# A fused decoder layer: block turns on VectorE over a DRAM scratch in place of TensorE transposes, and a longer second half of the last accumulation

## The chip, the cores and the metric

The kernel runs on one core of a Trainium2 chip. The metric is the device time of one execution in microseconds (us). All weights stream from DRAM once per execution; nothing is kept from one execution to the next.

## The reference, cut to what matters

One layer of a decoder on 256 tokens with 2048 features, in float32: a mixer (a state-space part and a gated short convolution), a cross-attention to 256 memory tokens, a SwiGLU block with 5632 hidden features, plain residual sums, and an RMS norm at the end.

```python
mem_n = rmsnorm(mem, mem_norm)
h = x
h = h + hybrid_mixer(rmsnorm(h, norm_mix), w_in, ..., w_out)        # ends with [y_ssd, y_sc] @ w_out
h = h + memory_cross_attention(rmsnorm(h, norm_xa), mem_n, w_q, w_k, w_v, w_o)
h = h + swiglu(rmsnorm(h, norm_ffn), w_gate, w_up, w_down)          # (silu(h @ w_gate) * (h @ w_up)) @ w_down
return rmsnorm(h, norm_final)
```

## The kernel before

**Products in two parts.** Each float32 operand is split into a rounded part `h` and a rest `l`, and a product is three matmuls: activation-h by weight-h, activation-h by weight-l, activation-l by weight-h (L796 to L798 in `tok_mm`).

**The weight stream.** All weights come as one list of chunks of 128x1024 (512 KB), in the order in which they are used. SP loads a chunk into one of six raw buffers (L151). ScalarE rounds it into one of four `hi` buffers (L165), and VectorE subtracts to give one of four `lo` buffers (L166). A raw buffer is free again when its `lo` is written; a `hi` or `lo` buffer is free when TensorE has used its chunk.

**Units and steps.** `unit` takes two chunks: it issues the loads up to five chunks past the unit, the splits that are still due, the matmuls of the first chunk, then calls `step()`, which lets every waiting post-process go on to its next `yield`, then the matmuls of the second chunk and one more load. So a `yield` puts off what follows by one unit. The orders of TensorE and SP are as written here (`manual_schedule`); those of ScalarE and VectorE come from a planner that simulates the program and takes what is ready.

**Stages around the change.** The mixer's output product (`wo`) runs over four column groups n of 512 features, 16 chunks each. After each, `wo_post` adds the product to the residual `res[tb][n]` (two token blocks of 128) and, one unit later, `to_features` turns it into features by tokens for the query product: eight TensorE transposes of 128x128 (L823) and a scaled split into slots (L179, L180). Then come queries, attention by head (`scores`, `turn`, `values`), the attention's output product, and eleven groups of gate and up products (`g`, `u`, eight chunks each). `u_post` multiplies the gate by the up product (L1008) and one unit later turns the result with eight transposes (L1015) and splits it (L1018, L1019) into `gs`, which is the stationary operand of the down product `d`, four column groups of 22 chunks.

**The end.** In the last two chunks of a column group of `d`, token block 0 runs first and then token block 1. For the last group `d_last` follows each: sums and squares (`d_sums`), the scale (`d_scale`), and the scaled output (`d_out`) written by eight transfers of 256 KB. Before the change the outputs of block 0 are issued in the call for block 1, after block 1's squares.

Of the kernel before, what the change touches and what calls it, by code (L numbers as in the profile page):

```python
# [13 lines left out]
F32 = mybir.dt.float32  # L14
F32R = mybir.dt.float32r
AF = mybir.ActivationFunctionType
ALU = mybir.AluOpType
# [3 lines left out]
T = 256  # L21
# [68 lines left out]
def trunk(tc, wst, vecs, xp, xtp, mp, wdt_in, nfin, outp):  # L90
    nc = tc.nc
# [8 lines left out]
    with ExitStack() as ctx:  # L100
# [5 lines left out]
        sp = E(tc.tile_pool(name="slots", bufs=65))  # L106
        tp = E(tc.tile_pool(name="tmp", bufs=8))
        gtp = E(tc.tile_pool(name="gate", bufs=4))
        accp = E(tc.tile_pool(name="acc", bufs=4, space=PSUM))
        mscp = E(tc.tile_pool(name="msc", bufs=4, space=PSUM))  # L110
        drp = E(tc.tile_pool(name="scr", bufs=1, space=DRAM))
# [18 lines left out]
        def msc():  # L130
            return mscp.tile([128, 512], F32, tag="m", name=nm("m"))
# [41 lines left out]
        def v(name, i):  # L173
            return vec[:, VOFF[name] + i:VOFF[name] + i + 1]

        def hilo_scaled(src, gain):

            a = slot(dt=F32R)
            act(a[:, 0:T], src, AF.Identity, scale=gain)  # L179
            stt(a[:, T:], src, gain, a[:, 0:T].bitcast(F32), ALU.mult, ALU.subtract)  # L180
            return a
# [631 lines left out]
                j = gtp.tile([128, 512], F32, tag="g", name=nm("j"))  # L813
                act(j, h, AF.Square, accum_out=sums[:, tb, n:n + 1])

        def to_features(n, gain, dst):

            for i in range(2):
                ps = msc()
                for f in range(2):  # L820
                    for tb in range(2):
                        o = (2 * i + f) * 128
                        nc.tensor.transpose(ps[:, f * T + tb * 128:f * T + tb * 128 + 128],  # L823
                                            res[tb][n][:, o:o + 128], ident)
                for f in range(2):
                    t = 4 * n + 2 * i + f
                    dst[t] = hilo_scaled(ps[:, f * T:f * T + T], v(gain, t))

        def token_scale(name, sums, factor=None):

# [13 lines left out]
        def wo_post(n, accs):  # L844
            add_to_res(n, accs, h1s)
            if n == 0:
                act(small("rv"), half, AF.Exp)
            if n == 3:
                xa["sc"] = token_scale("xsc", h1s, XSCALE)
            yield  # L850
            to_features(n, "nxa", h1g)

        for n in range(4):
            accs = [acc(), acc()]
# [41 lines left out]
        def turn(h):  # L896
            p, pt = ps_[h], msc()
            for mb in range(2):
                for lb in range(2):
                    nc.tensor.transpose(pt[:, mb * T + lb * 128:mb * T + lb * 128 + 128],  # L900
                                        p[:, lb * T + mb * 128:lb * T + mb * 128 + 128], ident)
            pts[h] = slot()
            nc.scalar.copy(pts[h], pt)

        def values(h):
            op = msc()
# [9 lines left out]
        def o_post(n, accs):  # L916
            add_to_res(n, accs, h2s)
            if n == 3:
                ff["r"] = token_scale("fscale", h2s)
            yield  # L920
            to_features(n, "nffn", h2g)

        oacc = {}

# [78 lines left out]
        def u_post(n, accs):  # L1003
            while n not in gate:
                yield
            for tb in range(2):
                s = gate[n][tb]
                stt(s, accs[tb], ff["r"][:, tb:tb + 1], s, ALU.mult, ALU.mult)  # L1008
            yield
            for i in range(2):  # L1010
                ps = msc()
                for f in range(2):
                    for tb in range(2):
                        o = (2 * i + f) * 128
                        nc.tensor.transpose(ps[:, f * T + tb * 128:f * T + tb * 128 + 128],  # L1015
                                            gate[n][tb][:, o:o + 128], ident)
                hi, lo = slot(dt=F32R), slot(dt=F32R)
                nc.scalar.copy(hi, ps)  # L1018
                tt(lo, ps, hi.bitcast(F32), ALU.subtract)  # L1019
                gs[2 * n + i] = hi, lo  # L1020

        def f_mm(accs, m, n, c):
# [45 lines left out]
                act(j[:, c], h[:, c], AF.Square, accum_out=ss[:, tb, 3 + i:4 + i])  # L1068

        def d_scale(tb):  # L1070
            h, r = res[tb][3], fr[:, tb:tb + 1]
            stt(r, ss[:, tb, 3:4], 1.0 / D, pre[:, tb:tb + 1], ALU.mult, ALU.add)
            stt(r, ss[:, tb, 4:5], 1.0 / D, r, ALU.mult, ALU.add)  # L1073
            gtt(r, r, half[:, 0:1], op=ALU.pow)  # L1074
            tt(h, h, gain[3], ALU.mult)

        def d_out(tb, ns):
            r = fr[:, tb:tb + 1]
            for n in ns:
                h = res[tb][n]  # L1080
                if n == 1:
                    act(h, h, AF.Identity, scale=r)
                else:
                    ts(h, h, r, None, ALU.mult)
                (nc.scalar if n % 2 else nc.sync).dma_start(outp[tb][:, n * 512:n * 512 + 512], h)

        def d_last(tb, ps):
            engines = {mybir.EngineType.Activation, mybir.EngineType.DVE, mybir.EngineType.Pool}
            with tc.manual_schedule(engines=engines):
                d_sums(tb, ps)  # L1090
                if tb == 0:
                    d_scale(0)
                else:
                    d_out(0, (0, 1, 2))
                    d_scale(1)
                    d_out(0, (3,))
                    d_out(1, (0, 1, 2, 3))

        def d_mm(ps, key, tbs, start, stop):
# [6 lines left out]
            tok_mm(ps, key, blocks, tbs, start, stop)  # L1106

        nd = FT // 2
        for n in range(4):
            accs = [acc(), acc()]  # L1110
            for c in range(0, nd - 2, 2):
                unit([([("d", n, k)], lambda k=k: d_mm(accs, ("d", n, k), (0, 1), k == 0, False))
                      for k in (c, c + 1)])
            tail = [("d", n, nd - 2), ("d", n, nd - 1)]

            def last_mm(tb):
                for key in tail:
                    d_mm(accs, key, (tb,), False, key == tail[1])
# [10 lines left out]
def _pairs(a):  # L1129
    import numpy as np  # L1130
    return np.ascontiguousarray(a.T.reshape(8, 2, 128, T).transpose(0, 2, 1, 3).reshape(8, 128, 512))


def _cols(a):
# [7 lines left out]
def _weights(i):  # L1142
    import numpy as np
    w_in = np.asarray(i["w_in"])[0]
    blk = {}

    def tiles(w, ck):
        k, n = w.shape
        return w.reshape(k // 128, 128, n // 128, 128).transpose(2, 1, 0, 3)

    blk["a"] = tiles(w_in[:, 0:5120], 8)
    blk["b"] = tiles(w_in[:, 5152:], 8)
    blk["q"] = tiles(np.asarray(i["w_q"])[0], 8)
    rows = {m: np.asarray(i[k])[0].reshape(-1, 2, 128, i[k].shape[-1] // 512, 512).transpose(3, 0, 2, 1, 4)
            for m, k in (("wo", "w_out"), ("o", "w_o"), ("g", "w_gate"), ("u", "w_up"), ("d", "w_down"))}
    wk, wv = np.asarray(i["w_k"])[0], np.asarray(i["w_v"])[0]
    plan = stream_plan()
    out = np.empty(sum(128 * w for _, w in plan), np.float32)
    p = 0
    for key, w in plan:  # L1160
        m = key[0]
        if m == "k0":
            c = wk[0:128]
        elif m == "v0":
            c = wv[0:128]
        elif m == "kv":
            s = slice(key[1] * 128, key[1] * 128 + 128)
            c = np.concatenate([wk[s], wv[s]], axis=1)
        elif m in rows:
            c = rows[m][key[1], key[2]]  # L1170
        else:
            c = blk[m][key[1]][:, 8 * key[2]:8 * key[2] + w // 128]
        out[p:p + 128 * w] = c.reshape(-1)
        p += 128 * w
    return out


def _vectors(i):
    import numpy as np
    g = {k: np.asarray(a) for k, a in i.items() if a.ndim <= 3}  # L1180
    part = {
        "nmix": _cols(g["norm_mix"][0]), "nmem": _cols(g["mem_norm"]), "nxa": _cols(g["norm_xa"][0]),
        "nffn": _cols(g["norm_ffn"][0]), "nssd": _cols(g["ssd_norm"][0]),
        "nsc": _cols(g["sc_norm"][0]), "cw": _cols(g["ssd_conv_w"][0].T), "cb": _cols(g["ssd_conv_b"][0]),
        "sw": _cols(g["sc_conv_w"][0].T), "dsk": _cols(np.repeat(g["d_skip"][0], 64)),
        "dtb": np.broadcast_to(g["dt_bias"][0], (128, H)), "alog": np.broadcast_to(g["a_log"][0], (128, H)),
    }
    return np.ascontiguousarray(np.concatenate([part[n] for n, _ in _W], axis=1))
# [33 lines left out]
```

## Time and profile before

| | us |
|---|---|
| median of 3 runs (1557.65 to 1558.63) | 1558.58 |
| the profiled execution | 1558.37 |
| span of its instructions | 1556.7 |
| TensorE busy / VectorE busy / ScalarE busy | 1541.9 / 916.8 / 805.3 |
| DMA, mean over the span | 193 GB/s |

The profile shows one execution. Its time is 1.7 us longer than the span, which goes from the first to the last instruction. Busy time of TensorE counts matmuls whose ends are modelled and which overlap; the distance between two starts tells what one costs.

### The profile page before, as it was taken

The numbers are of one execution on the slowest core, as the hardware profiler recorded it, in microseconds if no ns is written. First come the engines' busy times: TensorE is split into PE (matmuls) and PEld (weight loads), VectorE is DVE, ScalarE is ACT, GpSimd is POOL, SyncE is SP. The second block draws the span as 40 slices with busy tenths as digits, with TensorE's granted clock in tenths as the row PEclk, the third lists the DMA queues.
The fourth block names the chain that finished last, engine by engine and source line by source line (L and its number), as shares of the span: only waits on it lengthen the run. The fifth ranks groups of instructions, "written<-read, shape, count | busy, mean of one in ns | idle before, by whom it ended". The sixth has DMA issues, their size and how long they took to land.

```text
span 1556.7 us, 20300 instructions
## 1 busy us (share of the span) xinstructions
PE 1541.9 (99%) x7716; PEld 1294.6 (83%) x7716; DVE 916.8 (59%) x1214; ACT 805.3 (52%) x1157; POOL 46.6 (3%) x65
## 2 busy tenths in 40 slices
PE   9999999999999999999999999999999999999997
PEld 7888888888888888888888888888888888888886
DVE  5976886776776674555575555545455555455453
ACT  6685775774765454444465444444444444344342
POOL 0011300100000000000000000000000000000000
PEclk9999999999999999999999999999999999999999
DMA  9665655655655556665545555555555556656662
GB/s 346 248 199 192 217 173 181 209 183 173 220 170 183 173 186 199 203 202 202 191 134 183 189 184 193 189 197 189 189 189 188 183 194 209 201 191 195 194 191 95
DMA packets 92962, 300.66 MB, mean 193 GB/s; under 512 B 9888, under 2 KB 18496, under 8 KB 92864
## 3 DMA queue, kind: packets, MB, share of 16 engines
q1 hardware_dynamic: 83664, 291.98, 56.4%
q10 hardware_dynamic: 9200, 7.39, 1.6%
q8 instruction: 60, 0.98, 0.2%
q14 instruction: 38, 0.31, 0.1%
HBM read 297.19 MB, written 2.15 MB: 192 GB/s over the span
## 4 chain that ended last, share of the span: by engine, by line
PE 96%; DMA 2%; ACT 1%; DVE 0%; issue 0%; SPq 0%; POOLq 0%; POOL 0%; DVEq 0%; ACTq 0%
PE a L294 21%; PE a L796 20%; PE a L798 20%; PE a L797 20%; PE a L300 11%; DMA s<-in_m_dram 1%; PE m L1015 1%; PE m L674 1%; DMA r<-in_w_dram 0%; PE m L823 0%; PE m L200 0%; ACT h L165 0%; DMA s<-in_x_dram 0%; PE m L242 0%; PE a L516 0%
## 5 line engine op out<-in xcount | busy, mean ns | idle before, releaser
L166 DVE TENSOR_TENSOR l<-r,h 128x1024 fp32r<-128x1024 f32 (+2 forms) x555 | 657.2, 1193 | 537.0 <-ACT h L165 464.4
L165 ACT CAST h<-r 128x1024 fp32r<-128x1024 f32 (+2 forms) x555 | 564.5, 1022 | 629.2 <-PE a L798 475.3
L796 PE MATMUL a<-h,s 128*128 128x512 f32 x1344 | 525.7, 391 | 0.0
L798 PE MATMUL a<-h,s 128*128 128x512 f32 x1344 | 523.2, 389 | 0.0
L797 PE MATMUL a<-l,s 128*128 128x512 f32 x1344 | 523.0, 389 | 0.0
L294 PE MATMUL a<-s,h 128*128 128x512 f32 x1472 | 370.4, 397 | 0.3 <-ACT h L165 0.3
L294 PEld LDWEIGHTS a<-s,h 128*128 128x128 f32 x1472 | 265.5, 188 | 52.9 <-issue 2.6
L798 PEld LDWEIGHTS a<-h,s 128*128 128x128 f32 x1344 | 252.3, 188 | 52.8
L797 PEld LDWEIGHTS a<-l,s 128*128 128x128 f32 x1344 | 252.4, 188 | 51.7
L796 PEld LDWEIGHTS a<-h,s 128*128 128x128 f32 x1344 | 252.3, 188 | 51.3
L300 PEld LDWEIGHTS a<-s,l 128*128 128x128 f32 x1472 | 188.9, 191 | 7.8
L300 PE MATMUL a<-s,l 128*128 128x256 f32 x1472 | 191.4, 282 | 0.0
L192 ACT COPY t<-a 128x256 f32<-128x256 f32 x96 | 35.1, 369 | 36.9 <-PE a L300 36.6
L615 DVE SCALAR_TENSOR_TENSOR t<-t,vec,t 128x255 f32<-128x255 f32 (+2 forms) x72 | 34.9, 485 | 6.3 <-ACT t L612 5.5
L235 POOL TENSOR_TENSOR rr<-rv,half 128x2 f32<-128x2 f32 x24 | 16.6, 692 | 646.4 <-DVE rv L234 629.4
L193 DVE TENSOR_TENSOR t<-a,t 128x256 f32<-128x256 f32 x76 | 31.9, 419 | 5.0 <-ACT t L192 3.8
L516 PE MATMUL a<-s,h 128*128 128x512 f32 x64 | 25.1, 421 | 1.5 <-DVE s L180 1.4
L1074 POOL TENSOR_TENSOR fr<-fr,half 128x1 f32<-128x1 f32 x2 | 1.9, 942 | 726.7 <-DVE fr L1073 726.7
L1000 ACT ACTIVATE g<-a,fscale 128x512 f32<-128x512 f32 x22 | 15.0, 690 | 9.9 <-PE a L798 9.9
L517 PE MATMUL a<-s,l 128*128 128x256 f32 x64 | 18.6, 290 | 0.6 <-DVE l L166 0.6
L179 ACT ACTIVATE s<-m,vec 128x256 fp32r<-128x256 f32 x32 | 14.2, 470 | 9.4 <-DVE s L180 9.2
L616 ACT ACT_TABLE_LOAD x12 | 15.4, 1283 | 6.1 <-DVE t L615 3.1
(163 smaller groups left out, 680.8 us busy)
## 6 DMA issues: line engine op xcount, KB each, us to landing
r<-in_w_dram SPq DMA_DIRECT2D x535, 512.0 KB, 3.3
s<-acsT ACTq DMA_DIRECT2D x24, 256.0 KB, 6.1
s<-in_xt_dram SPq DMA_DIRECT2D x16, 256.0 KB, 5.7
s<-in_x_dram SPq DMA_DIRECT2D x8, 256.0 KB, 7.2
s<-in_m_dram SPq DMA_DIRECT2D x7, 256.0 KB, 7.2
s<-in_nfin_dram SPq DMA_DIRECT2D x4, 256.0 KB, 3.8
out_dram<-s SPq DMA_DIRECT2D x4, 256.0 KB, 3.1
out_dram<-s ACTq DMA_DIRECT2D x4, 256.0 KB, 3.7
```

The lines of the kernel that those rows point to most:

```text
L165: nc.scalar.copy(h[:, c], r[:, c])
L166: tt(l[:, c], r[:, c], h[:, c].bitcast(F32), ALU.subtract)
L192: nc.scalar.copy(t, ps[:, T:])
L193: tt(dst, ps[:, 0:T], t, ALU.add)
L294: mm(ps, h[:, k * 128:k * 128 + 128], acts[k0 + k], start=start and k == 0, stop=False)
L300: mm(ps[:, 0:T], l[:, k * 128:k * 128 + 128], acts[k0 + k][:, 0:T], start=False, stop=stop and k == n - 1)
L516: mm(kacc[t], h[:, t * 128:t * 128 + 128], a, start=s, stop=False)
L517: mm(kacc[t][:, 0:T], l[:, t * 128:t * 128 + 128], a[:, 0:T], start=False, stop=e)
L615: stt(a[:, d:], u[:, 0:T - d], v("cw", 4 * ct + k), a[:, d:], ALU.mult, ALU.add)
L796: mm(ps[tb], ah, h[:, w], start=start and i == ks[0], stop=False)
L797: mm(ps[tb], ah, l[:, w], start=False, stop=False)
L798: mm(ps[tb], al, h[:, w], start=False, stop=stop and i == ks[-1])
```

## The change

Three parts, and the packing of the weights to go with them.

1. **Turns.** For the eleven gate groups and for the first three residual groups, the eight TensorE transposes give way to: two VectorE transposes of 128x512, which turn every 32x32 block in itself (`turn_blocks`); one unit later one transfer of the 512 KB result to a scratch tensor in DRAM (`put`); one unit later four transfers of 128 KB back, 32 partitions each, in pieces of 512 bytes (`get`); one unit later the split, now from SBUF and not from PSUM. Features come out in another order inside each group of 512; the rows of `w_down` and `w_q` and the gain are packed in that order (`_turned`). The fourth residual group and the attention output's groups stay on TensorE.
2. **Attention.** The PSUM copy of the first head's turned scores goes from ScalarE to VectorE, with priority.
3. **The end.** In the last group, block 1 runs four chunks behind block 0 in place of two. Both blocks write their outputs in their own call. The gain of the last 512 features is multiplied together with the scale, outputs 0 and 3 are made by VectorE and issued by SP, 1 and 2 by ScalarE. The last chunk of block 1 is done in two column halves (`d_halves`).

```diff
+        bp = E(tc.tile_pool(name="blocks", bufs=2))
+        fp = E(tc.tile_pool(name="feat", bufs=2))
...
+        def turn_blocks(src):
+            t = bp.tile([128, 1024], F32, tag="b", name=nm("b"))
+            for tb in range(2):
+                nc.vector.transpose(t[:, tb * 512:tb * 512 + 512], src[tb])
+            return t
+
+        def put(t):
+            w = drp.tile([2, 128, 512], F32, tag="w", name=nm("w"), bufs=2)
+            nc.sync.dma_start(w.rearrange("t p k -> p t k"), t.rearrange("p (t k) -> p t k", t=2))
+            return w
+
+        def get(w):
+            d = fp.tile([128, 1024], F32, tag="f", name=nm("f"))
+            for b in range(4):
+                nc.sync.dma_start(d[32 * b:32 * b + 32, :].rearrange("p (x c) -> p x c", x=8),
+                                  w.rearrange("t (a i) k -> i (t a) k", a=4)[:, :, 128 * b:128 * b + 128])
+            return d.rearrange("p (x f j) -> p f x j", x=8, f=4)
+
+        def gained(src, gain, t):
+            a = slot(dt=F32R)
+            hi, lo = a[:, 0:T], a[:, T:]
+            if len(src.shape) == 3:
+                hi, lo = [o.rearrange("p (x j) -> p x j", x=8) for o in (hi, lo)]
+            act(hi, src, AF.Identity, scale=v(gain, t))
+            stt(lo, src, v(gain, t), hi.bitcast(F32), ALU.mult, ALU.subtract)
+            return a
+
-        def to_features(n, gain, dst):
+        def to_features(n, gain, dst, spare):
+            if spare:
+                t = turn_blocks([res[tb][n] for tb in range(2)])
+                yield
+                w = put(t)
+                yield
+                d = get(w)
+                yield
+                for f in range(4):
+                    dst[4 * n + f] = gained(d[:, f], gain, 4 * n + f)
+                return
...
-            to_features(n, "nxa", h1g)
+            yield from to_features(n, "nxa", h1g, n < 3)
...
-            nc.scalar.copy(pts[h], pt)
+            if h == 0:
+                with tc.high_priority():
+                    nc.vector.tensor_copy(pts[h], pt)
+            else:
+                nc.scalar.copy(pts[h], pt)
...
-            to_features(n, "nffn", h2g)
+            yield from to_features(n, "nffn", h2g, False)
...
                 stt(s, accs[tb], ff["r"][:, tb:tb + 1], s, ALU.mult, ALU.mult)
+            t = turn_blocks(gate[n])
+            yield
+            w = put(t)
+            yield
+            d = get(w)
             yield
             for i in range(2):
-                ps = msc()
-                for f in range(2):
-                    for tb in range(2):
-                        o = (2 * i + f) * 128
-                        nc.tensor.transpose(ps[:, f * T + tb * 128:f * T + tb * 128 + 128],
-                                            gate[n][tb][:, o:o + 128], ident)
                 hi, lo = slot(dt=F32R), slot(dt=F32R)
-                nc.scalar.copy(hi, ps)
-                tt(lo, ps, hi.bitcast(F32), ALU.subtract)
+                hv, lv = [a.rearrange("p (f x j) -> p f x j", f=2, x=8) for a in (hi, lo)]
+                nc.scalar.copy(hv, d[:, 2 * i:2 * i + 2])
+                tt(lv, d[:, 2 * i:2 * i + 2], hv.bitcast(F32), ALU.subtract)
                 gs[2 * n + i] = hi, lo
...
         def d_scale(tb):
-            h, r = res[tb][3], fr[:, tb:tb + 1]
+            r = fr[:, tb:tb + 1]
...
-            tt(h, h, gain[3], ALU.mult)
...
-                if n == 1:
+                if n in (1, 2):
                     act(h, h, AF.Identity, scale=r)
+                elif n == 3:
+                    stt(h, h, r, gain[3], ALU.mult, ALU.mult)
                 else:
                     ts(h, h, r, None, ALU.mult)
-                (nc.scalar if n % 2 else nc.sync).dma_start(outp[tb][:, n * 512:n * 512 + 512], h)
+                (nc.scalar if n in (1, 2) else nc.sync).dma_start(outp[tb][:, n * 512:n * 512 + 512], h)
...
                 d_sums(tb, ps)
-                if tb == 0:
-                    d_scale(0)
-                else:
-                    d_out(0, (0, 1, 2))
-                    d_scale(1)
-                    d_out(0, (3,))
-                    d_out(1, (0, 1, 2, 3))
+                d_scale(tb)
+                d_out(tb, (0, 1, 3, 2))
...
+        def d_halves(ps, key):
+            tok_mm({1: ps}, key, d_blocks(key), (1,), False, False, (0,))
+            h, l = fin(key)
+            ah, al = d_blocks(key)(1, 1)
+            for i in range(2):
+                c, w = slice(i * T, i * T + T), slice(512 + i * T, 512 + i * T + T)
+                mm(ps[:, c], ah, h[:, w], start=False, stop=False)
+                mm(ps[:, c], ah, l[:, w], start=False, stop=False)
+                mm(ps[:, c], al, h[:, w], start=False, stop=i == 1)
...
-            for c in range(0, nd - 2, 2):
+            nt = 2 if n < 3 else 4
+            for c in range(0, nd - nt, 2):
...
-            tail = [("d", n, nd - 2), ("d", n, nd - 1)]
+            tail = [("d", n, k) for k in range(nd - nt, nd)]
...
                 for key in tail:
-                    d_mm(accs, key, (tb,), False, key == tail[1])
+                    if n == 3 and tb == 1 and key == tail[-1]:
+                        d_halves(accs[1], key)
+                    else:
+                        d_mm(accs, key, (tb,), False, key == tail[-1])
...
+def _turned(a, n=None):
+    if n is not None:
+        return np.concatenate([_turned(a[:n * 512]), a[n * 512:]])
+    n, rest = a.shape[0] // 512, a.shape[1:]
+    return a.reshape((n, 4, 4, 32) + rest).swapaxes(1, 2).reshape((n * 512,) + rest)
...
-    nc = bacc.Bacc("TRN2", target_bir_lowering=False, num_devices=1)
+    nc = bacc.Bacc("TRN2", target_bir_lowering=False, num_devices=1, dynamic_dma_scratch_size=1024)
```

## Rows read from the trace of the kernel before

**Rows 1.** The page: busy time and share of the span, then the span in 40 slices (tenths of TensorE's busy time and of its granted clock).

```profile
PE 1541.9 (99%) x7716; PEld 1294.6 (83%) x7716; DVE 916.8 (59%) x1214; ACT 805.3 (52%) x1157; POOL 46.6 (3%) x65
...
PEclk9999999999999999999999999999999999999999
```

**Rows 2.** The page: the chain of work that ended last, by engine.

```profile
PE 96%; DMA 2%; ACT 1%; DVE 0%; issue 0%; SPq 0%; POOLq 0%; POOL 0%; DVEq 0%; ACTq 0%
```

**Rows 3.** The timeline of TensorE around the turns of the first, second and last gate group (start us, us until the last end, line).

```profile
870.22 0.39 PE L798 MATMUL a<-h,s 128*128 128x512 f32 x1
870.45 1.04 PE L1015 MATMUL m<-ident,g 128*128 128x128 f32 x8
871.24 0.48 PE L796 MATMUL a<-h,s 128*128 128x512 f32 x1
871.55 0.39 PE L797 MATMUL a<-l,s 128*128 128x512 f32 x1
...
914.88 1.04 PE L1015 MATMUL m<-ident,g 128*128 128x128 f32 x8
...
1314.72 1.04 PE L1015 MATMUL m<-ident,g 128*128 128x128 f32 x8
```

**Rows 4.** The timeline of ScalarE in the down product: the roundings of four chunks in a row, each released by TensorE.

```profile
1525.27 1.05 ACT L165 CAST h<-r 128x1024 fp32r<-128x1024 f32 x1 [1.67 <-PE a L798]
...
1533.43 1.05 ACT L165 CAST h<-r 128x1024 fp32r<-128x1024 f32 x1 [1.67 <-PE a L798]
```

**Rows 5.** The timeline of TensorE in the mixer's output product: the turns of residual groups 0 and 1, which stand 192 matmuls apart.

```profile
635.02 1.04 PE L823 MATMUL m<-ident,s 128*128 128x128 f32 x8
...
679.45 1.04 PE L823 MATMUL m<-ident,s 128*128 128x128 f32 x8
```

**Rows 6.** Groups by line, in the stretch from 833 to 1321 us (all gate and up groups): count, busy us, mean ns of one, idle time of the engine before it.

```profile
L166 DVE TENSOR_TENSOR l<-r,h 128x1024 fp32r<-128x1024 f32 x176 | 215.6, 1225 | 244.9 <-ACT h L165 244.9
...
L1008 DVE SCALAR_TENSOR_TENSOR g<-a,fscale,g 128x512 f32<-128x512 f32 x22 | 15.4, 744 | 0.0
...
L1018 ACT CAST s<-m 128x512 fp32r<-128x512 f32 x22 | 11.7, 586 | 0.0
L1015 PE MATMUL m<-ident,g 128*128 128x128 f32 x88 | 11.4, 272 | 0.0
```

**Rows 7.** The waits of SP in the same stretch (us in total, times, longest), and the time from issue to landing of its weight loads from 840 to 1300 us.

```profile
SPq L151 <- DVE l L166: 414.9, 176, 3.2
...
DMA to landing us min/median/max: 3.0/3.3/5.3
```

**Rows 8.** The timelines of VectorE, ScalarE and SP around the first gate group's product (its accumulation ends at about 862.3 us).

```profile
861.99 1.41 DVE L1008 SCALAR_TENSOR_TENSOR g<-a,fscale,g 128x512 f32<-128x512 f32 x2
863.57 1.23 DVE L166 TENSOR_TENSOR l<-r,h 128x1024 fp32r<-128x1024 f32 x1 [0.17 <-ACT h L165]
...
869.01 1.23 DVE L166 TENSOR_TENSOR l<-r,h 128x1024 fp32r<-128x1024 f32 x1 [1.50 <-ACT h L165]
...
867.92 1.05 ACT L165 CAST h<-r 128x1024 fp32r<-128x1024 f32 x1 [1.67 <-PE a L798]
870.65 1.05 ACT L165 CAST h<-r 128x1024 fp32r<-128x1024 f32 x1 [1.67 <-PE a L798]
...
870.26 14.84 SPq L151 DMA_DIRECT2D r<-in_w_dram  x6
```

**Rows 9.** Reads of another DRAM scratch in pieces of 512 bytes, 256 KB each, six of them and their like issued together (duration of the issue ns min/median/max, then time to landing), and the load of that queue from 0 to 600 us.

```profile
L582 ACTq DMA_DIRECT2D s<-acsT x8: 366/488/1234, 81.1 to 399.0; - x8
...
DMA to landing us min/median/max: 4.1/6.8/9.7
...
q10 hardware_dynamic: 8624, 6.34, 3.7%
```

**Rows 10.** VectorE on 128x512 float32 in SBUF: groups by line, means in ns.

```profile
L1052 DVE TENSOR_TENSOR s<-s,s 128x512 f32<-128x512 f32 x6 | 4.1, 690 | 2.4 <-ACT s L1051 2.4
...
L1084 DVE TENSOR_SCALAR s<-s,fr 128x512 f32<-128x512 f32 x6 | 2.6, 480 | 0.1
```

**Rows 11.** The timelines of TensorE, ScalarE and VectorE in the attention: the first head's turn, its copy, its value product, and the second head's scaling.

```profile
784.12 0.60 PE L900 MATMUL m<-ident,s 128*128 128x128 f32 x4
784.48 1.19 PE L300 MATMUL a<-s,l 128*128 128x256 f32 x8
786.62 1.13 PE L908 MATMUL m<-s,s 128*128 128x256 f32 x4 [0.95 <-ACT s L903]
787.58 0.60 PE L900 MATMUL m<-ident,s 128*128 128x128 f32 x4
...
785.99 0.57 ACT L903 COPY s<-m 128x512 f32<-128x512 f32 x1
...
786.57 0.62 DVE L893 TENSOR_SCALAR s<-s,sm 128x256 f32<-128x256 f32 x2
```

**Rows 12.** The timeline of the end (all engines), the time to landing of the eight output transfers, and the last us in windows (from:to, us, busy of PE, PEld, DVE, ACT, POOL, clock, DMA share, GB/s).

```profile
1546.61 0.39 PE L798 MATMUL a<-h,s 128*128 128x512 f32 x1
1547.03 0.76 DVE L1067 TENSOR_TENSOR s<-a,s 128x256 f32<-128x256 f32 x2 [0.56 <-PE a L798]
...
1548.99 0.96 POOL L1074 TENSOR_TENSOR fr<-fr,half 128x1 f32<-128x1 f32 x1 [2.11 <-DVE fr L1073]
...
1550.34 0.72 ACT L1082 ACTIVATE s<-s,fr 128x512 f32<-128x512 f32 x1 [1.33 <-POOL fr L1074]
...
L1085 ACTq DMA_DIRECT2D out_dram<-s x4: 338/375/572, 1549.0 to 1551.5; - x4
...
DMA to landing us min/median/max: 2.5/3.3/4.2
...
1549.00:1555.00 6.00, 0.00 (x0) 0.00 (x0) 2.18 (x5) 0.73 (x2) 0.94 (x1) 0.59 0.99 349
```

**Rows 13.** The same chain for token block 0, which ran undisturbed: first sum, and the power that ends its scale.

```profile
1544.31 0.76 DVE L1067 TENSOR_TENSOR s<-a,s 128x256 f32<-128x256 f32 x2 [5.85 <-PE a L798]
...
1545.95 0.93 POOL L1074 TENSOR_TENSOR fr<-fr,half 128x1 f32<-128x1 f32 x1 [724.59 <-DVE fr L1073]
```

**Rows 14.** The waits of ScalarE: the copy of one half of a PSUM bank (L192) and the matmuls into the other half (L300).

```profile
ACT t L192 <- PE a L300: 36.6, 44, 2.6
```

More of the change, by code (lines that the diff above doesn't have):

```diff
@@ L826, in to_features @@
                     t = 4 * n + 2 * i + f
-                    dst[t] = hilo_scaled(ps[:, f * T:f * T + T], v(gain, t))
+                    dst[t] = gained(ps[:, f * T:f * T + T], gain, t)
         def token_scale(name, sums, factor=None):
@@ L1090, in d_last, with d_blocks @@
                 d_sums(tb, ps)
-                if tb == 0:
-                    d_scale(0)
-                else:
-                    d_out(0, (0, 1, 2))
-                    d_scale(1)
-                    d_out(0, (3,))
-                    d_out(1, (0, 1, 2, 3))
-        def d_mm(ps, key, tbs, start, stop):
+                d_scale(tb)
+                d_out(tb, (0, 1, 3, 2))
+        def d_blocks(key):
             hi, lo = gs[key[2]]
@@ L1104, in blocks, with d_mm @@
                 return hi[:, o], lo[:, o]
-            tok_mm(ps, key, blocks, tbs, start, stop)
+            return blocks
+        def d_mm(ps, key, tbs, start, stop):
+            tok_mm(ps, key, d_blocks(key), tbs, start, stop)
+        def d_halves(ps, key):
[7 more added lines that the diff above has]
+                mm(ps[:, c], al, h[:, w], start=False, stop=i == 1)
         nd = FT // 2
@@ L1131, in _pairs @@
     return np.ascontiguousarray(a.T.reshape(8, 2, 128, T).transpose(0, 2, 1, 3).reshape(8, 128, 512))
+def _turned(a, n=None):
+    import numpy as np
+    if n is not None:
+        return np.concatenate([_turned(a[:n * 512]), a[n * 512:]])
+    n, rest = a.shape[0] // 512, a.shape[1:]
+    return a.reshape((n, 4, 4, 32) + rest).swapaxes(1, 2).reshape((n * 512,) + rest)
 def _cols(a):
@@ L1152, in _weights @@
     blk["b"] = tiles(w_in[:, 5152:], 8)
-    blk["q"] = tiles(np.asarray(i["w_q"])[0], 8)
-    rows = {m: np.asarray(i[k])[0].reshape(-1, 2, 128, i[k].shape[-1] // 512, 512).transpose(3, 0, 2, 1, 4)
+    blk["q"] = tiles(_turned(np.asarray(i["w_q"])[0], 3), 8)
+    rows = {m: (_turned(np.asarray(i[k])[0]) if m == "d" else np.asarray(i[k])[0]).reshape(-1, 2, 128, i[k].shape[-1] // 512, 512).transpose(3, 0, 2, 1, 4)
             for m, k in (("wo", "w_out"), ("o", "w_o"), ("g", "w_gate"), ("u", "w_up"), ("d", "w_down"))}
@@ L1181, in _vectors @@
     part = {
-        "nmix": _cols(g["norm_mix"][0]), "nmem": _cols(g["mem_norm"]), "nxa": _cols(g["norm_xa"][0]),
+        "nmix": _cols(g["norm_mix"][0]), "nmem": _cols(g["mem_norm"]), "nxa": _cols(_turned(g["norm_xa"][0], 3)),
         "nffn": _cols(g["norm_ffn"][0]), "nssd": _cols(g["ssd_norm"][0]),
```

## The prediction

> **What bounds the kernel.** [...] Busy time alone would not say what a removed matmul is worth, since busy times overlap: eight transposes of the first gate group start within 0.79 us, though one lasts 272 ns [rows 3, 6]. So I priced a group by distances. Neighbouring gate groups do the same 16 chunks of work; their turns stand 914.88 - 870.45 = 44.43 us apart, and from first to last (1314.72 - 870.45) / 10 = 44.43. In the down product, which has the same matmuls and no turns, three chunks take 1533.43 - 1525.27 = 8.16 us, so 2.72 us each [rows 4], and 16 chunks 43.52 us. Eight transposes therefore cost 44.43 - 43.52 = **0.91 us** of TensorE's order. The residual groups of the mixer's output product show the same 679.45 - 635.02 = 44.43 us for 192 matmuls [rows 5].
>
> Next, what feeds TensorE and with how much to spare. SP waits for a free raw buffer before every load (176 waits, 414.9 of 488 us), so the stream is held back by its buffers and not by DRAM [rows 7]. A load is issued when a `lo` is done (869.01 + 1.23 = 870.24, issue at 870.26); that chunk's rounding began at 867.92, and the load's own comes six chunks later, at 867.92 + 6 x 2.72 = 884.24. With 3.3 us to land, it has 10.7 us to spare [rows 7, 8]. A split starts when the chunk four before is used up, 8.16 us ahead of its need, and takes 870.24 - 867.92 = 2.32 us: 5.8 us to spare.
>
> **The turns.** 14 groups lose their transposes: 14 x 0.91 = **12.7 us**, if nothing that takes their place makes TensorE wait.
>
> VectorE gets two turns of 128x512 per group. No such operation is in the trace. The nearest rows, 512 float32 a partition out of SBUF, take 0.48 and 0.69 us [rows 10]; the far bound is the 1.23 us of an operation on 1024 elements [rows 6]. I take 0.69, since it is the general rate. VectorE idles 244.9 us before its splits in this stretch [rows 6], so 11 x 2 x 0.69 = 15 us fit; a split that is put off by one pair loses 1.4 of its 5.8 us. [...]
>
> SP gets five more transfers per group in its fixed order, and `put` waits for VectorE. By the loads issued ahead, SP comes to `put` about when the accumulation ends (862.3) or before; the two products end at 863.40 [rows 8] and the two turns at 864.8. So SP stands up to some 3 us, and again at the first `get`, until the data has landed in DRAM: 3.3 us as a 512 KB load [rows 7], so at 868.2. Behind SP stand only weight loads, with 10.7 us to spare; both stands and the issues (five of 0.37 to 0.49 us) stay near 5 us after what has caught up between them. Hidden. The engines' share grows little: a packet of the scratch's queue costs 0.037 x 16 x 600 / 8624 = 41 ns [rows 9], so 1024 pieces take 2.6 us of 16 engines, and with the `put` about 4 us in each 44.
>
> The return decides. Four gets are issued by 869.7; reads in 512-byte pieces landed in 4.1, 6.8, 9.7 us (least, median, most) when 1.5 MB went out together [rows 9]; here it is 0.5 MB, so I take 4.1 and the data at 873.8. ScalarE's copies wait for it, in order, with the splits behind them. In program order they stand ahead of the split of the chunk that TensorE starts at 870.45 + 5 x 2.72 = 884.05; two copies, rounding and subtraction (1.17 + 1.05 + 1.23) want 3.4 us, so the limit is **880.6**. If the planner puts the copies two splits earlier, where ScalarE idles before 870.65 [rows 8], the limit is 875.2. Both hold for 873.8. At the far bounds (turns behind a split, 866.0; landing 5.3; issues 2.0; landing 9.7) it would be 883.0, and neither holds.
>
> The copies' new source, SBUF in runs of 32 elements, has no row; at 0.59 us now [rows 6], even twice that costs ScalarE 1.2 us per group off the path.
>
> **The attention.** TensorE waits 0.95 us for ScalarE's copy, made at 785.99 behind two exponentials [rows 11]. VectorE is free from 784.6 and the transposes end near 784.7, so a copy of 0.69 us is done by 785.5 and the values start near 785.7. What is late next is the second head's turn, which needs VectorE's scaling, done at 787.19: it moves from 787.58 to 787.27. Gain **0.3 us**, between 0 and 0.95.
>
> **The end.** After the last matmul eight transfers of 256 KB share 6 us at 349 GB/s [rows 12]; half of them are block 0's. With two more chunks between (24 matmuls, 5.4 us) block 0's outputs are out before block 1's sums. Block 1's chain: first sum at 0, the power ends at 1545.95 + 0.93 - 1544.31 = 2.57 [rows 13]; now 1549.95 - 1547.03 = 2.92 [rows 12]. Then ScalarE makes and issues output 1 (0.72 + 0.38) and output 2 (the same), the last at about 4.5 with hand-overs. That is no sooner than now (1551.5 - 1547.03 = 4.47). What falls is the landing: with half the bytes, 2.5 to 3.3 us where the last now takes up to 4.2 [rows 12], so 0.9 to 1.7 us. I take **1.3 us**, and 0 as the far end. The halves of the last chunk give no head start: a copy of one half of a bank waits for matmuls into the other [rows 14]; six of 256 columns for three of 512 cost some 0.03 us.
>
> **Sum.** 12.7 + 0.3 + 1.3 - 0.03 = 14.3 us. From the profiled execution's 1558.37 (0.2 below the median): **1544.1 us**.
>
> **Rivals.**
> *The return is late, the kernel slower.* One mechanism: the copies of each group hold up ScalarE and the splits behind them, and TensorE waits 14 times. It decides at 880.6 us in the first group, a trip of 15.8 us from the `put`; no gain is left from 14.3 / 14 = 1.0 us later. At 883.0 the stall is 2.4 x 14 = 34 us: 1578. For it: the trip is two dependent transfers, and the slow reads of [rows 9]. Against: the median of those rows with the loads' 3.3 us gives 864.8 + 3.3 + 1.5 + 6.8 = 876.4, in time.
> *A part is given back.* The planner puts copies where ScalarE is idle, and with 876.4 against the limit of 875.2 some groups lose up to 1.2 us; at half of that, 8 us: about 1552. For it: ScalarE idles 1.67 us before each rounding. Against: 5.8 us lie in each split.
> *The pieces cost far more than the row's 41 ns*, because `get` reads 512 bytes out of every 2 KB row and not a row's whole length. To reach 880.6 from 873.8 they would have to take 2.6 + 6.8 = 9.4 us, 147 ns a piece; at 200 ns (12.8 us) each group is 3.4 us late, 48 us in all: 1592. For it: nothing in the trace reads across rows in this way. Against: [rows 9] have the same size of piece. [...]
> *TensorE's slots are not worth their distance*, because something else paces the stages: 1558. Against: the 44.43 us with turns and 43.52 without.
>
> **Chances.** The forecast 0.78, part given back 0.11, a late return 0.06, costly pieces 0.02, slots without worth 0.03. The forecast's own range is 12.7 + 0.95 + 1.7 = 15.3 off, 1543.0, to 12.7 off, 1545.7. The range that holds 8 in 10 adds half of the second rival: 1542.5 to 1549.0. A difference of 0.2% (3.1 us) is about what a measurement can tell from none. Faster: the forecast and the partial case, 0.89; same 0.03; slower 0.06 + 0.02 = 0.08.
>
> **What would show it.** Right: gate groups 43.5 us apart, no waits of TensorE between 600 and 1540 us; SP with waits for VectorE's turns and for the scratch, of a few us; `get` landing 8 to 10 us after the `put`'s issue; the last DMA bytes 1 us or more nearer to the last matmul; TensorE's gap at the first values gone, a smaller one at the second turn. Wrong: idle time of TensorE released by a rounding or a subtraction (return late), turns far over 0.69 us, or gate groups above 43.6 us with no wait.

## The result and the profile after

The changed kernel takes 1543.95 us (median of four runs, 1543.5 to 1545.01), the kernel before 1558.16 (four runs, 1557.65 to 1558.63): the ratio is 0.991, with a 95% interval of 0.9893 to 0.9927. The profiled execution took 1543.5 us with a span of 1541.8. The forecast was 1544.1.

The page of the changed kernel: busy time, the first queue of the weight stream, and the DMA issues of the turns beside the weight loads (KB each, median us to landing).

```profile
PE 1528.6 (99%) x7607; PEld 1282.6 (83%) x7607; DVE 930.3 (60%) x1239; ACT 807.0 (52%) x1158; POOL 44.9 (3%) x65
...
r<-in_w_dram SPq DMA_DIRECT2D x535, 512.0 KB, 4.1
w<-b SPq DMA_DIRECT2D x14, 512.0 KB, 3.3
f<-w SPq DMA_DIRECT2D x56, 128.0 KB, 4.4
```

TensorE is busy for the same 99% of a shorter span [rows 1], and the chain of work that ended last runs 95% through it (before: [rows 2]). Its waits from 560 us to the end (us in total, times, longest) are one line, and that is the attention's:

```profile
PE m L945 <- ACT s L187: 0.6, 1, 0.6
```

So no rounding, subtraction or copy of the turned data made TensorE wait in these stages. Where the 14.9 us between the spans went is read between fixed points of TensorE in both traces, first before and then after (the first matmul of `wo`, two small transposes of line L200, now L202, the turn of residual group 3, the attention's first output product):

```profile
582.59 0.40 PE L796 MATMUL a<-h,s 128*128 128x512 f32 x1
591.01 0.38 PE L200 MATMUL m<-ident,s 128*128 128x128 f32 x2
768.49 1.04 PE L823 MATMUL m<-ident,s 128*128 128x128 f32 x8
788.70 0.58 PE L796 MATMUL a<-h,s 128*128 128x512 f32 x1
```

```profile
581.77 0.40 PE L798 MATMUL a<-h,s 128*128 128x512 f32 x1
590.19 0.38 PE L202 MATMUL m<-ident,s 128*128 128x128 f32 x2
764.95 1.03 PE L868 MATMUL m<-ident,s 128*128 128x128 f32 x8
784.97 0.58 PE L798 MATMUL a<-h,s 128*128 128x512 f32 x1
```

| stretch | before | after | less |
|---|---|---|---|
| start to the first matmul of `wo` | 582.6 | 581.8 | 0.8 |
| from there to the two small transposes | 8.42 | 8.42 | 0.00 |
| from there to the turn of residual group 3 | 177.48 | 174.76 | 2.72 |
| from there to the attention's first output product | 20.21 | 20.02 | 0.19 |
| from there to the first sum of the end | 758.33 | 748.39 | 9.94 |
| first sum to the end of the span | 9.67 | 8.44 | 1.23 |

The first line is not the change: nothing ahead of `wo` was edited, and the same stretch lies between 581.8 and 583.5 us in all twelve runs below. In the tables below the time is therefore counted from the first matmul of `wo` to the end of the span: 974.1 us before, 960.0 after, 14.1 less. The third line spans the residual groups 0 to 2, the fifth the eleven gate groups: 2.72 + 9.94 = 12.66 us for 14 groups, 0.90 each.

The first gate group of the changed kernel: the timelines of VectorE, of SP and of ScalarE (start us, us, instructions in a row; in brackets the idle time before and its releaser).

```profile
858.28 1.40 DVE L1057 SCALAR_TENSOR_TENSOR g<-a,fscale,g 128x512 f32<-128x512 f32 x2
859.60 1.29 DVE L822 STREAM_TRANSPOSE b<-g 128x512 f32<-128x512 f32 x2
...
860.92 0.38 SPq L828 DMA_DIRECT2D w<-b  x1
861.39 1.30 SPq L153 DMA_DIRECT2D r<-in_w_dram  x2
864.11 1.81 SPq L836 DMA_DIRECT2D f<-w  x4
866.01 11.75 SPq L153 DMA_DIRECT2D r<-in_w_dram  x6
...
872.37 1.05 ACT L167 CAST h<-r 128x1024 fp32r<-128x1024 f32 x1 [1.67 <-PE a L800]
873.33 1.14 ACT L1067 CAST s<-f 128x512 fp32r<-128x512 f32 x2
875.09 1.06 ACT L167 CAST h<-r 128x1024 fp32r<-128x1024 f32 x1 [0.63 <-PE a L800]
```

The turns end at 860.89, the `put` goes out 0.03 us later, the first `get` 3.2 us after that, when the `put` has landed. The four `get` transfers land 4.7 to 5.8 us after their issue, the last at 865.46 + 5.75 = 871.21, and the copies run at 873.33. They fill the 1.67 us in which ScalarE otherwise waits for TensorE: the next rounding starts at 875.09, 2.72 us after the one before, as always. So the copies cost the splits nothing. The landing isn't the same in every group. These are the least, median and longest of the first gate group and of the last one, whose reads share the queue with the loads of the final gain:

```profile
DMA to landing us min/median/max: 4.7/5.1/5.8
...
DMA to landing us min/median/max: 7.8/8.4/8.5
```

The last group's copies are the only ones that wait for their data, for 1.3 us, and TensorE doesn't feel it.

The waits of SP over the whole run (us in total, times, longest):

```profile
SPq L153 <- DVE l L168: 1064.9, 426, 8.4
SPq L828 <- DVE b L822: 54.8, 14, 4.9
...
SPq L836 <- DMA w<-b: 16.2, 12, 1.6
```

SP stands 54.8 / 14 = 3.9 us for the turns and 1.35 us for the scratch, in a queue that stands 1064.9 us for free raw buffers. And the stretch of the gate groups in one window (us; busy of PE, PEld, DVE, ACT, POOL; clock; DMA share; GB/s):

```profile
833.00:1300.00 467.00, 467.00 (x2062) 386.71 (x2061) 248.96 (x236) 206.32 (x215) 0.00 (x0) 1.00 0.66 215
```

The same window before:

```profile
833.00:1300.00 467.00, 467.00 (x2102) 387.45 (x2102) 231.35 (x209) 202.52 (x212) 0.00 (x0) 1.00 0.57 190
```

The DMA share rose from 0.57 to 0.66: 0.09 x 43.5 = 3.9 us more of the engines per group.

### The profile page after: what moved, and what is told of

Same layout as the page of the kernel before. It is cut to its first block, busy times and chain, and to the rows that moved or that the text cites. A ratio compares the mean times of both kernels' runs of the same rounds, so it can differ in the third digit from the quotient of the medians.

```text
span 1541.8 us, 20228 instructions
## 1 busy us (share of the span) xinstructions
PE 1528.6 (99%) x7607; PEld 1282.6 (83%) x7607; DVE 930.3 (60%) x1239; ACT 807.0 (52%) x1158; POOL 44.9 (3%) x65
## 4 chain that ended last, share of the span: by engine, by line
PE 95%; DMA 1%; ACT 1%; issue 1%; SPq 0%; DVE 0%; POOLq 0%; POOL 0%; ACTq 0%
PE a L296 22%; PE a L800 20%; PE a L799 20%; PE a L798 20%; PE a L302 11%; DMA r<-in_w_dram 1%; PE m L676 1%; ACT h L167 0%; PE m L202 0%; PE m L244 0%; PE a L518 0%; PE m L868 0%; PE m L678 0%; PE m L660 0%; PE m L926 0%
## 5 line engine op out<-in xcount | busy, mean ns | idle before, releaser
L236 DVE TENSOR_SCALAR rv<-rv 128x2 f32<-128x2 f32 x24 | 4.0, 168 | 24.4 <-ACT t L229 24.1
```

## The experiments

The rival to be told from the forecast is in each case named in the expectation. "Counted time" is from the first matmul of `wo` to the end of the span.

**The parts alone.** `e1_turns_only` is the changed kernel with the attention copy and the end of before; `e2_end_only` and `e3_attention_only` are the kernel before with one part each.

```diff
# e3_attention_only, against before
-            nc.scalar.copy(pts[h], pt)
+            if h == 0:
+                with tc.high_priority():
+                    nc.vector.tensor_copy(pts[h], pt)
+            else:
+                nc.scalar.copy(pts[h], pt)
# e2_end_only, against before: d_scale, d_out, d_last, d_halves and the tail of the changed kernel
# e1_turns_only, against the changed kernel: these and the attention copy as before
```

> The changed turns alone; attention copy and end as before. Theory (TensorE's slots are the gain): 14 groups x 0.91 us = 12.7 us off, so a span near 1556.7 - 12.7 = 1544.0 and a time near 1545.6 (a start up to 1 us sooner or later left aside), gate groups 43.5 us apart, TensorE with no wait after 600 us. Rival (the end carries a good part, the turns give some back): span above 1546.

> The kernel before with the changed end alone. Theory: from the first sum of block 1 to the end of the span 9.67 us become 8.4, 1.2 to 1.3 us off, of which part is the landing of the last output (4.2 us before, 3.5 at most now) and part a shorter chain to the scale (2.92 before, about 2.2). Rival (the end is bound by a fixed latency after the last issue, the shorter stretch was chance): under 0.5 us off.

> The kernel before with the first head's copy on VectorE alone. Theory: the values of the first head start 0.95 us sooner, the turn of the second head only 0.3 us sooner, since it waits for VectorE's scaling; from the first head's turn to the first matmul of the attention's output product 4.58 us become 4.3 to 4.4. Rival (the copy was the only late thing): 3.6 us.

Measured: the turns alone 1545.4 us, ratio 0.9917 (0.9903 to 0.993), counted time 961.2, 12.9 less. The end alone 1557.31 against 1558.34, ratio 0.9994 (0.9985 to 1.0002), which the interval cannot tell from none; in its trace the counted time is 1.1 less. The attention alone, a single run of 1557.43: from the first head's turn to its first output matmul 4.37 us, where before took 788.70 - 784.12 = 4.58, 0.21 less; its one wait of TensorE is the 0.6 us that the changed kernel shows. 12.9 + 1.1 + 0.2 = 14.2 against 14.1 together: the parts add up, and none takes from another.

**The slots back.** `e4_slots_back` keeps the whole way over the scratch and lets TensorE do the eight transposes as well, into a bank that nobody reads.

```diff
+        def old_turns(src):
+            for i in range(2):
+                ps = msc()
+                for f in range(2):
+                    for tb in range(2):
+                        o = (2 * i + f) * 128
+                        nc.tensor.transpose(ps[:, f * T + tb * 128:f * T + tb * 128 + 128], src[tb][:, o:o + 128], ident)
...
             t = turn_blocks(gate[n])
             yield
+            old_turns(gate[n])
```

> The changed kernel, with the eight TensorE transposes of each of the 14 groups issued again beside the new path; what they write is read by nobody. Theory (the gain is the slots of TensorE and nothing else in these stages): 12.7 us come back, gate groups 44.4 us apart, a span near 1541.8 + 12.7 = 1554.5. Rival (the gain is a shorter way for ScalarE and VectorE, no PSUM reads, fewer PSUM buffers in use): under 6 us come back.

Measured: 1557.36 us, ratio 0.9993 (0.9984 to 1.0003). The counted time is 972.6, 12.6 more than the changed kernel's. Its first two gate groups on TensorE:

```profile
870.53 1.03 PE L831 MATMUL m<-ident,g 128*128 128x128 f32 x8
...
914.96 1.04 PE L831 MATMUL m<-ident,g 128*128 128x128 f32 x8
```

They stand 44.43 us apart again, as in [rows 3]. With the slots back, all of the turns' gain is gone while VectorE, SP and the DMA do as in the changed kernel. So the gain is TensorE's slots, 12.6 / 14 = 0.90 us a group, and nothing else.

**Two edits of the end.** `e5_gain_back` multiplies by the gain on VectorE beside the power, as before; `e6_no_halves` does the last chunk in whole columns.

```diff
# e5_gain_back
             gtt(r, r, half[:, 0:1], op=ALU.pow)
+            tt(res[tb][3], res[tb][3], gain[3], ALU.mult)
...
-                elif n == 3:
-                    stt(h, h, r, gain[3], ALU.mult, ALU.mult)
# e6_no_halves
-                    if n == 3 and tb == 1 and key == tail[-1]:
+                    if False:
```

> The changed kernel with the multiplication of the last 512 features by their gain put back on VectorE beside the scale's power on GpSimd; output 3 is then only scaled. Before, the power took 0.93 and 0.96 us, in the changed kernel 0.55. Theory: GpSimd is held up by VectorE's operation on two SBUF tensors that runs at the same time, so the power takes 0.93 us again and comes 0.4 us later. Rival (the power's time depends on what it is given or on the place of the buffers): 0.55 us.

> The changed kernel with the last chunk of block 1 in full columns. Theory (a reader of half a bank waits for all matmuls into the bank): from the last full matmul of the chunk before to the first sum nothing is lost, some 0.03 us are won. Rival (the halves let the first sum start early): 0.3 us lost.

Measured, one run each: 1544.78 and 1543.51 us. The power in the changed kernel, and then VectorE and GpSimd in `e5_gain_back`:

```profile
1535.00 0.55 POOL L1123 TENSOR_TENSOR fr<-fr,half 128x1 f32<-128x1 f32 x1 [4.92 <-DVE fr L1122]
```

```profile
1535.77 0.68 DVE L1124 TENSOR_TENSOR s<-s,s 128x512 f32<-128x512 f32 x1
1535.93 0.93 POOL L1123 TENSOR_TENSOR fr<-fr,half 128x1 f32<-128x1 f32 x1 [4.54 <-DVE fr L1122]
```

The same instruction on one element a partition takes 0.55 us by itself and 0.93 beside VectorE's product of two SBUF tensors; first sum to end goes from 8.44 to 1543.1 - 1534.29 = 8.81 us. That is 0.37 of the end's 1.23. As to the halves, the changed kernel and `e6_no_halves`, last whole matmul and first sum of each:

```profile
1532.23 0.39 PE L800 MATMUL a<-h,s 128*128 128x512 f32 x1
...
1533.36 0.75 DVE L1116 TENSOR_TENSOR s<-a,s 128x256 f32<-128x256 f32 x2 [2.10 <-PE a L1165]
```

```profile
1532.26 0.39 PE L800 MATMUL a<-h,s 128*128 128x512 f32 x1
...
1533.36 0.76 DVE L1116 TENSOR_TENSOR s<-a,s 128x256 f32<-128x256 f32 x2 [2.07 <-PE a L800]
```

In both, one more chunk of block 1 lies between the two lines: 1.13 us in halves, 1.10 whole. In the changed kernel the first sum is one group of two instructions behind the last matmul of the second half, so the first half gets no start of its own. The halves cost 0.03 us in the trace, and a median would not show it.

**The trip, made harder.** `e7_one_step` issues `put` and `get` right behind the turns, so that SP stands for both in one place; `e8_small_pieces` reads back in 16 transfers of 32 KB, in pieces of 128 bytes.

```diff
# e7_one_step
-            t = turn_blocks(gate[n])
-            yield
-            w = put(t)
-            yield
-            d = get(w)
-            yield
+            d = get(put(turn_blocks(gate[n])))
+            yield
+            yield
+            yield
# e8_small_pieces
-                nc.sync.dma_start(d[32 * b:32 * b + 32, :].rearrange("p (x c) -> p x c", x=8),
-                                  w.rearrange("t (a i) k -> i (t a) k", a=4)[:, :, 128 * b:128 * b + 128])
+                for f in range(4):
+                    o = 128 * b + 32 * f
+                    nc.sync.dma_start(d[32 * b:32 * b + 32, 256 * f:256 * f + 256].rearrange("p (x j) -> p x j", x=8),
+                                      w.rearrange("t (a i) k -> i (t a) k", a=4)[:, :, o:o + 32])
```

> The changed kernel with put and get in SP's order right behind the turns, two units earlier. SP then comes to them some 8 us before the product is there, and stands for it and for the scratch's landing together 12 to 15 us in each group, against 4 and 1 now. Theory (16 us lie between a load's issue and TensorE's need of it: 10.7 of the load, 5.8 of the split): no or only small waits of TensorE, under 1 us a group, 0 to 14 us in all. Rival (any long stand of SP costs its length beyond a few us): 8 us a group and more, over 100 us.

> The changed kernel with the way back in pieces of 128 bytes in place of 512: sixteen transfers of 32 KB per group, 4096 pieces. Theory (41 ns a piece on one of 16 engines, whatever its size): 10.5 us of all engines per group in place of 2.6, data 8 to 10 us later, about at the limit of ScalarE's place for the copies; between 0 and 3 us a group, 0 to 40 us in all. Rival (pieces cost by their bytes): engines as busy as now and no change. Rival (small pieces out of long rows cost a multiple, 147 ns and more): 38 us of engines in each 44 us, loads late, over 150 us in all.

Measured: 1544.53 us, ratio 0.9913 (0.9884 to 0.9942), and 1544.35, ratio 0.9912 (0.9883 to 0.994), two runs each; neither trace has a wait of TensorE but the attention's. SP's waits and one of ScalarE's copies in `e7_one_step`:

```profile
SPq L828 <- DVE b L822: 131.6, 14, 10.3
...
SPq L836 <- DMA w<-b: 33.7, 14, 2.4
```

```profile
869.87 1.14 ACT L1063 CAST s<-f 128x512 fp32r<-128x512 f32 x2 [2.92 <-DMA f<-w]
```

SP stands (131.6 + 33.7) / 14 = 11.8 us a group and ScalarE waits up to 3.4 us for the data, and all of it is covered by the loads ahead. The weight queue from 833 to 1300 us (packets, MB, share of 16 engines), of the changed kernel and of `e8_small_pieces`:

```profile
q1 hardware_dynamic: 38404, 100.17, 66.0%
```

```profile
q1 hardware_dynamic: 71010, 100.20, 65.4%
```

32,606 more packets for the same bytes leave the engines' share where it was. The share alone is too coarse for the price of a piece, though: in `e7_one_step`, with pieces of 512 bytes, it is 60.9% in the same window (99.08 MB). The records of the single packets in the traces of this window tell more. In the changed kernel the 10,240 pieces of 512 bytes took 41.6 ns each on average, 26.6 us of 16 engines; in `e8_small_pieces` the 40,960 pieces of 128 bytes took 12.8 ns each, 32.8 us. So 41 ns whatever the size, the theory, is refuted, and so is the multiple: with a quarter of the bytes a piece took 0.31 of the time, so mostly by its bytes. But the small pieces aren't free; they take 0.6 us more of the engines per group, which the share doesn't show because the loads' packets of 4,096 bytes took a little less (185 in place of 192 ns). The 128-byte pieces took more for the same bytes, 102 ns a KB against 83; the loads' 4,096-byte packets took 48 beside the pieces of 512 bytes, so these moved their bytes at a lower rate than the loads did. A weight load's median landing rose from 3.3 to 4.4 us, but it is 4.9 in `e7_one_step`, so the small pieces need not be the cause.

**The same way where there is less slack.** The attention's output product is followed by the gate product at once, and its turned residual is the first operand of it. `e9_three_more` turns groups 1 to 3 of it by the scratch as well (rows and gain packed to fit), `e10_four_more` group 0 too, `e11_three_more_own_queue` is the first of them with these three groups' transfers issued by GpSimd. `e0_changed_again` is the changed kernel beside them.

```diff
# e9_three_more (e10_four_more: n >= 0; e11_three_more_own_queue: put and get on nc.gpsimd)
+            if n >= 1:
+                d = get(put(turn_blocks([res[tb][n] for tb in range(2)])))
+                yield
+                for f in range(4):
+                    h2g[4 * n + f] = gained(d[:, f], "nffn", 4 * n + f)
+                return
             yield
             yield from to_features(n, "nffn", h2g, False)
```

> The changed kernel itself, to be compared with the next two on the same chip: near 1544.0 us, 14.2 us below the kernel before.

> The changed kernel with three more groups turned in the new way: groups 1 to 3 of the attention's residual, which the gate and up products use soon after; turns, put and get stand in one step right behind the sum, the splits one step later. By the trace of the changed kernel, group n's data should land some 10.5 us after its accumulation ends and be split 2 us later, while TensorE needs it 15 to 16 us after. Theory (TensorE's slots are the gain while the way back is in time): 3 x 0.91 = 2.7 us off against the changed kernel, no wait of TensorE in that stage. Rival (in this stage VectorE and ScalarE are too full, and SP's stands come three times in 20 us): waits of TensorE for a split of the weights or for the features that eat the gain.

> As the one before, with group 0 too, which the very first gate matmul needs. Its features should be split some 12 us after its accumulation ends, about when TensorE comes to them. Theory: 3.6 us less whatever TensorE waits for group 0, between 0 and 2 us, so 1.6 to 3.6 off against the changed kernel. Rival: the wait is over 3 us, since the transfers share the queue with the weights, and nothing is won over three groups or over the changed kernel.

> The kernel with three more groups, but put and get of these three are issued by GpSimd, which has nothing else to do there, and not by SP. Before, with SP, the three more groups cost 3.2 us against the changed kernel instead of winning 2.7: TensorE waited 4.6 us, SP stood 39 us for turns and landings, and a put behind two weight loads took 5 to 6 us to land. Theory (what made the return late is SP's one order, in which loads, put and get stand for each other): SP no longer stands, TensorE waits under 1 us there, 1 to 2.7 us less than the changed kernel's 14 us gain over before, so 15 to 17 us below before. Rival (two dependent transfers are too long for this stage on any queue): TensorE still waits 3 us and more, 10 to 12 us below before.

| kernel | us | ratio to before | 95% interval |
|---|---|---|---|
| `e0_changed_again` | 1544.62 | 0.9914 | 0.99 to 0.9927 |
| `e9_three_more` | 1547.79 | 0.9938 | 0.9926 to 0.995 |
| `e10_four_more` | 1554.66 | 0.9978 | 0.997 to 0.9987 |
| `e11_three_more_own_queue` | 1555.44 | 0.9979 | 0.997 to 0.9988 |

Three groups fewer on TensorE, 2.7 us of its slots, made the kernel 3.2 us slower, so the theory of `e9_three_more` failed; with a fourth group it is 10.0 us, and TensorE waits 8.5 us in seven waits for roundings, subtractions and the features themselves. `e9_three_more` on SP, ScalarE and TensorE where the gate product begins:

```profile
811.09 0.38 SPq L828 DMA_DIRECT2D w<-b  x1
816.61 1.81 SPq L836 DMA_DIRECT2D f<-w  x4
818.52 0.87 SPq L153 DMA_DIRECT2D r<-in_w_dram  x2
819.48 0.38 SPq L828 DMA_DIRECT2D w<-b  x1
826.21 1.81 SPq L836 DMA_DIRECT2D f<-w  x4
828.06 20.57 SPq L153 DMA_DIRECT2D r<-in_w_dram  x13
...
831.62 1.71 ACT L846 ACTIVATE s<-f,vec 128x256 fp32r<-128x256 f32 x4 [5.63 <-DMA f<-w]
833.23 2.02 ACT L167 CAST h<-r 128x1024 fp32r<-128x1024 f32 x2
...
830.76 0.39 PE L800 MATMUL a<-h,s 128*128 128x512 f32 x1
834.31 0.80 PE L798 MATMUL a<-h,s 128*128 128x512 f32 x1 [3.16 <-ACT h L167]
```

The last `put` is issued at 819.48, behind two loads, and its `get` at 826.21: 6.7 us, where a gate group's `get` followed its `put` by 3.2. ScalarE's scaled copies wait 5.63 us, the roundings stand behind them, and TensorE waits 3.16 us for a rounding. This is the prediction's first rival at work: a weight chunk comes late because the copies hold up ScalarE. Then the clock (windows of `e9_three_more`, columns as above; this profiled execution, 1549.75 us, was the slowest of the five):

```profile
830.00:834.00 4.00, 1.15 (x6) 0.61 (x4) 1.68 (x4) 2.38 (x5) 0.00 (x0) 0.91 0.99 383
834.00:838.00 4.00, 3.22 (x7) 2.23 (x8) 3.65 (x4) 3.36 (x4) 0.00 (x0) 0.50 1.05 402
838.00:842.00 4.00, 4.00 (x15) 3.17 (x14) 1.51 (x2) 1.48 (x2) 0.00 (x0) 0.73 0.99 373
```

After the 3.2 us of idleness the granted clock is 0.50, and matmuls start 0.43 us apart (836.16, 836.59, ...) up to 840.0; from 840.3 on they stand 0.23 apart again. From 830.76 to 840.31 there are 13 starts in 9.55 us, which at 0.227 us would take 2.95: 6.6 us are lost, of which 3.16 + 0.46 are waits and 3.0 the clock and the restart. The profiled execution's counted time is 965.5, 5.5 above the changed kernel's 960.0: 6.6 and two more waits of 0.9 together make 7.5, less 2.7 for the slots 4.8; 0.7 us stay open.

`e11_three_more_own_queue` came out 2.8 us below before, worse than its theory (15 to 17) and its rival (10 to 12). With GpSimd's queue SP no longer stands for these groups, and yet TensorE waits 8.6 us in three waits for the scaled copies: GpSimd issued the eight `get` transfers of the last two groups one by one from 822.35 to 832.90. So to take these transfers out of SP's order in this way is no cure, though the run doesn't show what SP's order costs by itself, since the other queue brought slow issues of its own. On either queue, as tried, the trip is too long for this stage. Whether a larger `dynamic_dma_scratch_size` or an earlier turn would save it wasn't tried.

## Why the prediction was right, point by point

**TensorE's slots.** 14 x 0.91 = 12.7 us was the main term; the trace gives 12.66, and `e1_turns_only` and `e4_slots_back` 12.9 and 12.6 from either side. That the distance of starts is the price, and not the duration, is borne out: the 112 transposes at 272 ns [rows 6] would be 30 us.

**The turns on VectorE.** Taken as 0.69 us; the 22 of the gate groups take 0.684 and the six of the residual 0.701. Of the three rows in question [rows 6, 10], that of an operation with two inputs of 512 elements was the right one.

**SP.** Its stands and issues together were put at near 5 us a group. They are 3.9 + 1.35 of stands and 0.38 + 1.81 of issues, 7.4 us: too low a term, but hidden; with stands of 11.8 us in `e7_one_step` they still are.

**The return.** The `put` landed in 3.3 us (taken 3.3), the `get` in 4.4 (taken 4.1), both medians. In the first gate group, which the prediction worked out, the last `get` took 5.75. The changed kernel is 3.7 us ahead here (0.8 + 2.72 + 0.2 of the table); data at 871.2 + 3.7 = 874.9 answers to the predicted 873.8, 1.1 us later. The limit was set too strictly: the planner put the copies behind the rounding that I had them stand ahead of, one split of 2.72 us later, so the limit was 880.6 + 2.72 = 883.3. It did not put them earlier, which was the way to the second rival; its limit of 875.2 would have held by only 0.3 us, so here the forecast had some luck.

**The pieces.** The estimate of about 4 us of the engines per group was right (3.9 by the share). By the packet records the 1024 pieces at 41.6 ns make 2.7 us and a `put` 1.7. That the price fits is luck: the 41 ns of [rows 9] is a mean over 4,096 packets of 512 bytes, 28.8 ns each, and 4,096 of 1,024 bytes, 57.1 ns each; beside the weight loads the 512-byte ones happened to take 41.6. The rival of 200 ns a piece has no trace here. With the elements of a block turned by VectorE first, a read across rows landed in 4.4 us (the median of 56).

**The attention.** 0.3 us predicted. The second turn came 0.32 us sooner, as worked out (3.46 to 3.14 us behind the first); 0.12 of it went in a slower second turn (0.56 us for its four transposes, 783.73 to 784.29, in place of 0.44), and 0.2 remained.

**The end.** 1.3 us predicted, 1.23 measured, but not by the terms named, so the closeness is luck. The prediction had the last issue at 4.5 us after the first sum, no sooner than before, and all the gain in the landing. Measured: the last issue at 1537.47 - 1533.36 = 4.11, 0.36 sooner than the 4.47 of before, and the rest, 0.87, behind it, 0.7 of which is the longest landing, from 4.2 to 3.5. The step that was missed is the power: taken over as 0.93 us from [rows 13], and 0.55 once the gain's product no longer ran beside it. Nor were block 0's outputs out before block 1's sums: its last one landed at 1535.50, 2.1 us behind the first sum, though ahead of block 1's first issue at 1536.10.

## What to carry to other kernels

Where one engine is full and paced by its own starts, price what is taken from it by the distance between equal stages with it and without it. Work that leaves that engine may take a long way round, here 12 us over DRAM in place of 0.9 us on TensorE, as long as its slack is longer: read the slack from how far ahead the stage behind it runs, for each stage anew. Where the slack was short the same edit cost more than it saved (3.2 us slower in `e9_three_more`), and there, in the one execution that was profiled, the lower clock behind the wait (granted 0.50, 3.0 us beside 3.6) nearly doubled the loss.

## What the runs showed of the hardware

- Reads from DRAM in pieces of 512 bytes took 41.6 ns a piece on average beside the weight loads, in pieces of 128 bytes 12.8: for the same bytes 32.8 us of the 16 engines in place of 26.6. A load's packet of 4,096 bytes took 185 to 192 ns.
- GpSimd's operation on 128x1 took 0.55 us alone and 0.93 beside VectorE's product of two SBUF tensors (`e5_gain_back`).
- A transfer of 512 KB to DRAM with no load just ahead of it landed in 3.3 us (the median of the changed kernel's 14); behind two loads of the same size in its queue (`e9_three_more`) the read that waits for it went out 5.5 and 6.7 us after its issue.
- Behind a wait of 3.2 us in `e9_three_more` TensorE's granted clock was 0.50 from 834 to 838 us, and matmuls started 0.43 us apart until 840.0, in place of 0.227.
